# SwiGLU by seven products: where the sums of weight blocks are formed, and where 1/rms is applied

## The chip, the cores and the metric

One core of one Trainium2 chip runs the whole kernel in one launch. The metric is the device time in microseconds of that launch. Before the change three runs took 1748.85 us in the median (1747.3 to 1749.6).

## The reference, cut to what matters

The kernel computes one step of a one-layer decoder for 1024 prompt tokens and 32 sample tokens (T = 1056), model width 1024. The change concerns its last sublayer and the final norm:

```python
def rmsnorm(x, g):
    y = xf * lax.rsqrt(jnp.mean(xf * xf, axis=-1, keepdims=True) + EPS)
    return y * g
def swiglu_ffn(x, g_ffn, w_gate, w_up, w_down):      # D_FF = 2816 = 22 x 128
    h = rmsnorm(x, g_ffn)
    return x + (jax.nn.silu(h @ w_gate) * (h @ w_up)) @ w_down
y = rmsnorm(swiglu_ffn(x, ...), g_final)
```

All of it is float32. Each product is made of three passes of TensorE: both operands are split into a high part (rounded to the format in which TensorE takes 32-bit numbers) and a low rest, and high x high, high x low and low x high are added.

## The kernel before, in words

Data lie with channels on the 128 partitions and tokens along the free axis, so x is 8 blocks of 128 x 1056. The sublayer before leaves x in DRAM (`x3T`) and g x x, split, in SBUF (`x3`); 1/rms of each token, copied to all partitions, is `rbc`. It is applied after the products.

The hidden units are 22 tiles of 128 (f = 0 to 21). `first()` computes tile 0 in the ordinary way. The others go by the seven-product form of Strassen and Winograd: the weights of gate (row 1) and up (row 2), cut in two halves of the width, are four blocks a11, a12, a21, a22 of 128 x 512; the operand, cut in two halves of the width and two halves of the tokens (HT = 528), is B11, b12, B21, B22. Of the weights three sums are needed besides the plain blocks, s1 = a21 + a22 (for product P5), s2 = s1 - a11 (P6), and a11 - a21 (P7), and a12 - s2 (P3); of the operand T1 to T4, made once by `xsums` and `xsums_late` from x read back from DRAM (`xrload`), and each split by `Op.put`. P1 = a11 B11, P2 = a12 B21, P3 = (a12 - s2) B22, P4 = a22 T4, P5 = s1 T1, P6 = s2 T2, P7 = (a11 - a21) T3. One product is 24 matmuls of 264 columns (K = 4 blocks x 3 passes x 2 token quarters).

The down product uses the same form for hidden tiles 0 to 17 (`w_down4`, three groups of three pairs, 12 output tiles "b", K = 3, 18 matmuls a product); the last four tiles and the final norm follow in the ordinary way, in four blocks of tokens, at the end of the body (L1740 on).

`steps` (L1689 on) is the list of products in order: the first two tiles by turns, then one tile at a time in the order P1, P6, P5, P7, P2, P3, P4, then again by turns. Before product s, `ensure(s + 4)` calls `prepare` for the products up to four ahead: GpSimd forms the sum where one is needed (L1497, L1498, L1503, L1509), ScalarE copies the high part (L1517), VectorE subtracts for the low part (L1518, "a split"). The split blocks live in a ring of four (`pslots`), so the fourth one ahead waits for the product before. After the product, `aevac` takes the result from PSUM: P7's two operations (L1572, L1573) read the banks of P7 and P5; P3 and P2 add onto banks that still hold P5 and P1. After P4 the up half is multiplied by 1/rms (L1583) and by the gate half (L1584), both on GpSimd, and `spill` forms the operand sums of the down product for each pair of tiles and stores them to DRAM (`aD`, by GpSimd's DMA queue). The down stage fetches them (`build`, `Op.fetch`, L1387 to L1389) and adds its results onto x (`bevac`, L1631, L1643), which `xsload` reads from `x3T`.

Raw weight blocks are loaded by `pump` (L1485) on the SyncE queue into pages of 128 columns; a block of gate and up takes four pages, one of down three. There are two buffers of 16 pages.

The order of the work: the instructions of the SyncE queue run in the order of the program. Those of all other engines are ordered ahead of time by a planner, which simulates the program with its own costs and takes, on each engine, the ready instruction that is earliest in the program; on the chip each engine then runs its list in that order and waits where it must. `later(n, fn)` and `tick()` put small work, such as 1/rms, behind a number of units of matmuls.

Of the kernel before, what the change touches and what calls it, by code (L numbers as in the profile page):

```python
# [16 lines left out]
P = 128  # L17
# [13 lines left out]
NPAIR, NGRP = 9, 3  # L31
CK = 0.5 * 128.0 ** -0.5
# [105 lines left out]
def body(tc, ctx, I, O):  # L138
# [200 lines left out]
    def rstd(sqs, n, rcol, rbc):  # L339
# [5 lines left out]
        def by_token():  # L345
# [8 lines left out]
            vec.tensor_scalar(v[:, :full], pb[:, :full], 1.0 / D, EPS, ALU.mult, ALU.add)  # L354
            if n % P:
                m = n % P
                vec.tensor_scalar(v[:m, full:full + 1], pb[:m, full:full + 1], 1.0 / D, EPS, ALU.mult, ALU.add)
            y = newton(v[:, :len(tiles)], len(tiles))
# [3 lines left out]
        def over_all(n0=0, size=n):  # L362
            pb = PS[:, 7, :size]
            for j, (o, m) in enumerate(tiles):
                if n0 <= o < n0 + size:
                    mm(pb[:, o - n0:o - n0 + m], y[:m, j:j + 1].to_broadcast([m, P]), ident[:m, :m], True, True)
            act.copy(rbc[:, n0:n0 + size], pb)
# [719 lines left out]
    sqa = ar.take(T)  # L1087
    def residual(xin, src, spill, xout, g, blocks, at_once=False):
# [231 lines left out]

    sqa.drop()
# [92 lines left out]

    def xsums(k):
        x, (t1, t2) = xr[k % 2], (tt2[k % 2][:, a] for a in range(2))
        for a in range(2):
            act.activation(x[:, a], x[:, a], AF.Copy, scale=col(C_GF + k + 4 * a))
# [5 lines left out]
        if k >= 2:  # L1424
            gp.tensor_tensor(x[:, 1, :HT], x[:, 1, :HT], t2, ALU.subtract)
        else:
            ops[T3].put(k, x[:, 0, HT:])
# [3 lines left out]
    def xsums_late():  # L1431
# [5 lines left out]
        for k in (2, 3):  # L1437
            ops[T3].put(k, xr[k % 2][:, 0, HT:])
        for k in (2, 3):
            ops[T4].put(k, xr[k % 2][:, 1, :HT])  # L1440
        for k in (0, 1):
            (h1_, l1_), (h2_, l2_) = ops[B21].ap(k), ops[T2].ap(k)
            a, b = part(U, 2 + k, HT), part(cs, k, HT)
            eng = gp if k else vec
            eng.tensor_tensor(a, h1_, h2_, ALU.subtract)
            eng.tensor_tensor(b, l1_, l2_, ALU.subtract)
            eng.tensor_tensor(a, a, b, ALU.add)
            ops[T4].put(k, a, eng)
# [4 lines left out]
    pages = [(b, i) for b in range(2) for i in range(16)]  # L1453
    wants, held = [], {}

    def room(n):

        for x in pages:
            run = [(x[0], x[1] + i) for i in range(n)]
            if all(y in pages for y in run):  # L1460
                pages[:] = [y for y in pages if y not in run]
# [3 lines left out]
    def at(run):  # L1465
        return wraw[run[0][0]][:, P * run[0][1]:P * (run[-1][1] + 1)]

    def leave(run):
        pages[:] = sorted(pages + run)

    def quarter(kind, i, c, k):

        if kind == "a":
            return I[("w_gate", "w_up")[c]][i][:, 4 * k:4 * k + 4]
        return I["w_down4"][i // 4, i % 4][:, k, c]
# [428 lines left out]
```

## Time and profile before

| | |
|---|---|
| median of three runs | 1748.85 us |
| the profiled execution's own time | 1751.22 us |
| its span | 1749.4 us |
| TensorE (PE) busy | 1678.4 us, 96% |
| VectorE (DVE) busy | 1197.4 us, 68% |
| ScalarE (ACT) busy | 691.9 us, 40% |
| GpSimd (POOL) busy | 572.0 us, 33% |
| mean granted clock of TensorE | 0.981 |
| DMA | 208.03 MB |

The span is the time of the instructions on the chip in one profiled execution; the metric holds a little around it. Busy times are sums over an engine's instructions. A granted clock of 1.0 is the upper of TensorE's two levels, 2.4 GHz, and 0.5 the lower; values between are means over a stretch. The sublayer of the change runs from about 989 us to the end.

### The profile page before, as it was taken

The numbers are of one execution on the slowest core, as the hardware profiler recorded it, in microseconds if no ns is written. First come the engines' busy times: TensorE is split into PE (matmuls) and PEld (weight loads), VectorE is DVE, ScalarE is ACT, GpSimd is POOL, SyncE is SP. The second block draws the span as 40 slices with busy tenths as digits, with TensorE's granted clock in tenths as the row PEclk, the third lists the DMA queues.
The fourth block names the chain that finished last, engine by engine and source line by source line (L and its number), as shares of the span: only waits on it lengthen the run. The fifth ranks groups of instructions, "written<-read, shape, count | busy, mean of one in ns | idle before, by whom it ended". The sixth has DMA issues, their size and how long they took to land. (4 is left out here: it accounts for less than half of the span.)

```text
span 1749.4 us, 32149 instructions
## 1 busy us (share of the span) xinstructions
PE 1678.4 (96%) x12540; PEld 1604.1 (92%) x12540; DVE 1197.4 (68%) x2536; ACT 691.9 (40%) x1396; POOL 572.0 (33%) x509
## 2 busy tenths in 40 slices
PE   6999999999999899999999979999999997999997
PEld 6989999999869899989989979999999997999987
DVE  7787777777638744666554496777677778787666
ACT  5463543543515543344343342222222225244244
POOL 3200100101101323200004375766676653332434
PEclk9999999999999999999999989999999998999999
DMA  5113112112244664475444513222223335544122
GB/s 177 62 34 82 52 55 91 52 51 83 96 148 133 224 205 141 151 241 200 157 147 144 181 38 117 93 92 93 93 98 104 119 106 196 183 156 132 29 101 97
DMA packets 89306, 208.03 MB, mean 119 GB/s; under 512 B 10466, under 2 KB 38018, under 8 KB 89026
## 3 DMA queue, kind: packets, MB, share of 16 engines
q1 hardware_dynamic: 76434, 163.32, 28.5%
q0 software_dynamic: 12720, 42.65, 6.9%
q8 instruction: 99, 1.62, 0.4%
q14 instruction: 53, 0.43, 0.1%
HBM read 158.93 MB, written 47.00 MB: 118 GB/s over the span
## 5 line engine op out<-in xcount | busy, mean ns | idle before, releaser
L266 PE MATMUL banks<-g_all 128*128 128x384 f32 (+7 forms) x4512 | 740.0, 315 | 10.4 <-DVE g_all L415 8.5
L266 PEld LDWEIGHTS banks<-g_all 128*128 128x128 f32 (+1 forms) x4512 | 671.9, 190 | 35.0 <-issue 17.3
L1539 PE MATMUL banks<-g_all 128*128 128x264 f32 x4120 | 560.3, 287 | 22.7 <-DVE f_all L1599 6.6
L1539 PEld LDWEIGHTS banks<-g_all 128*128 128x128 f32 x4120 | 533.6, 191 | 25.0 <-DVE f_all L1599 6.8
L1517 ACT CAST g_all<-f_all 128x512 fp32r<-128x512 f32 (+1 forms) x231 | 134.0, 581 | 358.8 <-PE banks L1539 312.1
L1518 DVE TENSOR_TENSOR g_all<-f_all,g_all 128x512 fp32r<-128x512 f32 (+1 forms) x231 | 237.4, 1036 | 12.7 <-ACT g_all L1517 12.7
L1539 PE MATMUL banks<-g_x,g_all 128*128 128x264 f32 x920 | 168.3, 288 | 8.5 <-DVE g_all L1518 8.5
L1539 PEld LDWEIGHTS banks<-g_x,g_all 128*128 128x128 f32 x920 | 137.4, 192 | 9.2 <-DVE g_all L1518 9.1
L225 DVE TENSOR_TENSOR g_all<-f_all,g_all 128x1024 fp32r<-128x1024 f32 x88 | 109.6, 1247 | 40.9 <-ACT g_all L224 40.4
L224 ACT CAST g_all<-f_all 128x1024 fp32r<-128x1024 f32 x88 | 91.9, 1048 | 96.5 <-PE banks L266 46.5
L1497 POOL TENSOR_TENSOR f_all<-f_all 128x512 f32<-128x512 f32 (+1 forms) x33 | 44.1, 1335 | 151.9 <-DMA f_all<-in_w_down_dram 65.3
L266 PE MATMUL banks<-f_x 128*128 128x129 f32 (+8 forms) x606 | 91.5, 307 | 1.4 <-DVE f_x L726 0.9
L266 PEld LDWEIGHTS banks<-f_x 128*128 128x128 f32 (+4 forms) x606 | 67.1, 159 | 14.9 <-issue 5.7
L1583 POOL TENSOR_TENSOR f_y<-f_y,f_all 128x1056 f32<-128x1056 f32 x21 | 59.4, 2828 | 61.0 <-DVE f_y L1582 61.0
L266 PE MATMUL banks<-g_y,g_all 128*128 128x384 f32 (+1 forms) x432 | 77.6, 323 | 0.0
L1098 DVE TENSOR_TENSOR f_all<-banks,f_all 128x384 f32<-128x384 f32 (+1 forms) x48 | 25.1, 523 | 73.8 <-PE banks L266 73.7
L266 PEld LDWEIGHTS banks<-g_y,g_all 128*128 128x128 f32 x432 | 70.5, 188 | 0.0
L266 PE MATMUL banks<-g_x,g_all 128*128 128x384 f32 (+1 forms) x336 | 70.2, 325 | 0.0
L661 POOL DMA_DIRECT2D mixT<-f_all x23 | 12.9, 562 | 154.6 <-ACT f_all L660 140.6
L266 PEld LDWEIGHTS banks<-g_x,g_all 128*128 128x128 f32 x336 | 57.0, 188 | 0.5 <-issue 0.4
L1099 POOL DMA_DIRECT2D x3T<-f_all x24 | 13.4, 558 | 131.4 <-DVE g_x L1252 84.0
L266 PE MATMUL banks<-f_all 128*32 128x256 f32 (+5 forms) x404 | 42.0, 347 | 14.8 <-DVE f_all L336 6.4
(410 smaller groups left out, 2212.8 us busy)
## 6 DMA issues: line engine op xcount, KB each, us to landing
g_all<-aD SPq DMA_DIRECT2D x48, 264.0 KB, 3.9
f_all<-in_w_mq_dram SPq DMA_DIRECT2D x24, 512.0 KB, 4.3
f_all<-in_w_gate_dram SPq DMA_DIRECT2D x42, 256.0 KB, 2.7
f_all<-in_w_up_dram SPq DMA_DIRECT2D x42, 256.0 KB, 2.7
f_all<-in_w_cm_dram SPq DMA_DIRECT2D x20, 512.0 KB, 3.6
aD<-f_y POOLq DMA_DIRECT2D x18, 528.0 KB, 4.9
f_all<-in_w_down_dram SPq DMA_DIRECT2D x48, 192.0 KB, 3.2
f_all<-in_memK_dram SPq DMA_DIRECT2D x16, 512.0 KB, 5.2
```

Of the source, the lines that this page charges most:

```text
L224: act.copy(R(dst_hi), raw)
L225: eng.tensor_tensor(R(dst_lo), raw, dst_hi, ALU.subtract)
L266: pe.matmul(out, l, r, start=start, stop=stop)
L661: gp.dma_start(mixT[:, 4 + i, P * t:P * t + P], ot)
L1098: vec.tensor_tensor(x, pb[:, :n], t, ALU.add)
L1099: gp.dma_start(spill[:, k, n0:n0 + n], x)
L1497: gp.tensor_tensor(s1, a21, a22, ALU.add)
L1517: act.copy(R(hi), src)
L1518: vec.tensor_tensor(R(lo), src, hi, ALU.subtract)
L1539: pe.matmul(o, x[:, k], R(y[:, n]), start=k == 0 and i == 0 and not more, stop=k == K - 1 and i == 2, skip_group_check=more)
L1583: gp.tensor_tensor(u, u, rbc.ap, ALU.mult)
```

## The change

Three things are changed. (1) The signs of the seven-product form are turned so that all sums of weight blocks are additions (T1 to T3 change sign instead, and the evacuations subtract where they added). The sums are then formed by DMAs that add to what lies at their destination, issued from GpSimd's queue: P5's block is loaded plain with a21 and a22 is added to it; P7's with a11 and a21 is added; P6's with a11 and the finished block of P5 is added, from SBUF to SBUF; P3's with a12 and the finished block of P6 is added. Each product has pages of its own, and the scratch `stmp` of the old sums becomes a third buffer of 16 pages; two of the three are handed out only after the first block of tokens of `first()`. (2) The up half is no longer multiplied by 1/rms. The residual is divided by it instead (`xdivide`, 16 pieces of 128 x 528, one after P5 of each of the tiles 3 to 18, through DRAM to `xS`), so that x / r + down product is r times too small, and the final 1/rms is computed with r taken into account (`times` in `rstd`, from columns saved by `final_by_token`). (3) What GpSimd still did in the loops of this sublayer (operand sums, product of the halves, sums of the spill, last sums of the down stage) goes to VectorE; the operand rows k = 0 and 1 are read from DRAM a second time for it. The sums of squares and one output block of the last part stay on GpSimd.

```diff
@@ rstd
+            parts = [(P, slice(0, full))] + ([(n % P, slice(full, full + 1))] if n % P else [])
+            for m, c in parts:
+                if times is None:
+                    vec.tensor_scalar(v[:m, c], pb[:m, c], 1.0 / D, EPS, ALU.mult, ALU.add)
+                else:
+                    vec.scalar_tensor_tensor(v[:m, c], pb[:m, c], 1.0 / D, times[1][:m, c], ALU.mult, ALU.mult)
...
+            if times is not None:
+                vec.tensor_scalar(v, v, 1.0, EPS, ALU.mult, ALU.add)
+            y = newton(v, len(tiles))
+            if times is not None:
+                vec.tensor_tensor(y, y, times[0][:, :len(tiles)], ALU.mult)
@@ before residual
+    def final_by_token():
+        rfin = fr["y"], fr["y2"] = [ar.take(12)[:, :frow[-1]] for _ in range(2)]
+        pb = PS[:, 7, 496:496 + frow[-1]]
+        for j, (o, m) in enumerate(t for b in ftiles for t in b):
+            mm(pb[:, j:j + 1], sqa[:, o:o + P], one[:, 0:1], True, True)
...
+    def final_over(j):
...
+        act.copy(rbc[:, n0:n0 + n], pb)
@@ residual
         if at_once:
-            by_token, over_all = rstd([sqa[:, :T]], T, None, rbc[:, :T])
-            later(1, by_token)
-            for j, b in enumerate(blocks):
-                later(j + 2, lambda b=b: over_all(*b))
+            later(1, final_by_token)
+            for j in range(len(FBL)):
+                later(2 + j // 2, lambda j=j: final_over(j))
@@ xsums, xsums_late
-        vec.tensor_tensor(t1, x[:, 0, HT:], x[:, 0, :HT], ALU.subtract)
-        gp.tensor_tensor(x[:, 0, HT:], x[:, 1, HT:], x[:, 0, HT:], ALU.subtract)
-        vec.tensor_tensor(t2, x[:, 1, HT:], t1, ALU.subtract)
+        xscale(k)
+        vec.tensor_tensor(t1, x[:, 0, :HT], x[:, 0, HT:], ALU.subtract)
+        vec.tensor_tensor(t2, x[:, 1, HT:], t1, ALU.add)
         ops[T2].put(k, t2)
         ops[T1].put(k, t1)
...
+        for k in (2, 3, 0, 1):
+            x = xr[k % 2]
+            if k < 2:
+                xscale(k)
+            vec.tensor_tensor(x[:, 0, HT:], x[:, 0, HT:], x[:, 1, HT:], ALU.subtract)
+            ops[T3].put(k, x[:, 0, HT:])
+            vec.tensor_tensor(x[:, 1, :HT], x[:, 1, :HT], x[:, 0, :HT], ALU.subtract)
+            vec.tensor_tensor(x[:, 1, :HT], x[:, 1, :HT], x[:, 0, HT:], ALU.add)
+            ops[T4].put(k, x[:, 1, :HT])
+            if k >= 2:
+                xrload(k - 2)
@@ pages, pump, prepare
-    pages = [(b, i) for b in range(2) for i in range(16)]
+    pages = [(wraw[1], i) for i in range(16)]
...
+            put(sy, quarter(*{P1: (0, 0), P6: (0, 0), P7: (0, 0), P2: (0, 1), P3: (0, 1), P5: (1, 0), P4: (1, 1)}[p]))
+            more = {P5: (1, 1), P7: (1, 0)}.get(p)
+            if more:
+                put(gp, quarter(*more), accum_op=ALU.add)
+            other = {P6: P5, P3: P6}.get(p)
+            if other is not None:
+                put(gp, at(held[kind, i, other]).rearrange("p (k c) -> p k c", c=P), accum_op=ALU.add)
...
+        run = held.pop((kind, i, p))
         b = pslots.next()
         hi, lo = b[:, :n], b[:, 512:512 + n]
-        act.copy(R(hi), src)
-        vec.tensor_tensor(R(lo), src, hi, ALU.subtract)
+        act.copy(R(hi), at(run))
+        vec.tensor_tensor(R(lo), at(run), hi, ALU.subtract)
+        leave(run)
         pump()
@@ spill
-            gp.tensor_tensor(c1, e[:, HT:], e[:, :HT], ALU.subtract)
-            vec.tensor_tensor(c2, u[:, HT:], c1, ALU.subtract)
-            gp.tensor_tensor(e[:, HT:], u[:, HT:], e[:, HT:], ALU.subtract)
+            vec.tensor_tensor(c1, e[:, :HT], e[:, HT:], ALU.subtract)
+            vec.tensor_tensor(c2, u[:, HT:], c1, ALU.add)
+            vec.tensor_tensor(e[:, HT:], e[:, HT:], u[:, HT:], ALU.subtract)
             vec.tensor_tensor(c3, u[:, :HT], c2, ALU.subtract)
@@ aevac, P4
-            gp.tensor_tensor(u, u, rbc.ap, ALU.mult)
-            gp.tensor_tensor(u, g, u, ALU.mult)
+            vec.tensor_tensor(u, g, u, ALU.mult)
@@ first
-            vec.tensor_tensor(bu, pu[:, :n], rbc[:, o], ALU.mult)
-            gp.tensor_tensor(u[:, o], z, bu, ALU.mult)
+            vec.tensor_tensor(u[:, o], pu[:, :n], z, ALU.mult)
+            if j == 0:
+                for b in (stmp.ap, wraw[0]):
+                    leave([(b, i) for i in range(16)])
@@ new, and called after P5 of the tiles 3 to 18
+    def xdivide(j):
+        x, n = part(cs, 3, HT), slice(HT * (j % 2), HT * (j % 2) + HT)
+        sy.dma_start(x, x3T[:, j // 2, n])
+        inv = part(ur, j % 2, HT)
+        vec.reciprocal(inv, rbc[:, n])
+        vec.tensor_tensor(x, x, inv, ALU.mult)
+        gp.dma_start(xS[:, j // 2, n], x)
+
     def xsload(d):
-        sy.dma_start(xsb[d], x3T[:, d])
+        sy.dma_start(xsb[d], xS[:, d])
@@ bevac
-                gp.tensor_tensor(x, x, u2, ALU.add)
+                vec.tensor_tensor(x, x, u2, ALU.subtract if p == P3 else ALU.add)
@@ last_ready
-            if wholes_free >= 2 and not wants and len(pages) >= 16:
+            if wholes_free >= 2 and not wants:
@@ body
+            if p == P5 and 3 <= i < 19:
+                xdivide(i - 3)
...
-        by_token, over_all = rstd(sqs, n, None, r)
+        by_token, over_all = rstd(sqs, n, None, r, [fr[x][:, frow[b]:] for x in ("y", "y2")])
```

## Rows read from the trace of the kernel before

**Rows 1.** The page: span, and busy us of each engine (share, instructions).

```profile
span 1749.4 us, 32149 instructions
PE 1678.4 (96%) x12540; PEld 1604.1 (92%) x12540; DVE 1197.4 (68%) x2536; ACT 691.9 (40%) x1396; POOL 572.0 (33%) x509
```

**Rows 2.** Busy time by stretch: length, engines' busy us (instructions), clock, DMA share, GB/s.

```profile
1017.00:1048.00 31.00, 18.51 (x120) 18.27 (x120) 30.11 (x29) 13.42 (x22) 20.97 (x13) 0.78 0.00 1
1048.00:1455.00 407.00, 402.76 (x3300) 401.83 (x3300) 292.94 (x316) 116.95 (x182) 258.87 (x160) 1.00 0.31 106
1455.00:1500.00 45.00, 32.85 (x209) 31.70 (x208) 40.20 (x46) 20.74 (x36) 20.29 (x14) 0.81 0.57 185
1500.00:1677.00 177.00, 174.57 (x1419) 173.83 (x1417) 126.34 (x192) 61.91 (x115) 60.80 (x51) 0.99 0.37 120
1677.00:1687.40 10.40, 7.26 (x35) 7.04 (x36) 7.10 (x11) 5.92 (x9) 1.49 (x2) 0.67 0.60 216
1300.00:1350.00 50.00, 50.00 (x412) 50.00 (x412) 35.83 (x38) 15.00 (x23) 32.59 (x20) 1.00 0.24 82
```

**Rows 3.** TensorE's waits from 985 us on: for what, us in total, times, longest.

```profile
PE banks L1539 <- DVE g_all L1518: 14.1, 6, 5.9
PE banks L1539 <- DVE f_all L1599: 6.6, 1, 6.6
PE banks L1539 <- DVE f_y L1573: 5.7, 5, 2.0
PE banks L1539 <- DVE f_y L1572: 4.9, 1, 4.9
```

**Rows 4.** VectorE's groups, 1050 to 1450: count, busy us, mean ns, idle before, releaser.

```profile
L1518 DVE TENSOR_TENSOR g_all<-f_all,g_all 128x512 fp32r<-128x512 f32 x132 | 161.1, 1233 | 9.7 <-ACT g_all L1517 9.7
L1580 DVE SCALAR_TENSOR_TENSOR f_all<-f_all 128x1056 f32<-128x1056 f32 x19 | 28.1, 1481 | 2.0 <-ACT f_all L1579 2.0
L1575 DVE TENSOR_TENSOR f_all<-banks,f_all 128x528 f32<-128x528 f32 x19 | 13.4, 706 | 13.3 <-PE banks L1539 13.3
```

**Rows 5.** GpSimd's groups, 1050 to 1450, the costliest.

```profile
L1583 POOL TENSOR_TENSOR f_y<-f_y,f_all 128x1056 f32<-128x1056 f32 x19 | 54.9, 2887 | 48.0 <-DVE f_y L1582 48.0
```

**Rows 6.** Line 1518, whole span: count, duration ns min/median/max, first and last start.

```profile
L1518 DVE TENSOR_TENSOR g_all<-f_all,g_all x231: 543/684/5757, 1012.2 to 1670.4; 128x512 fp32r<-128x512 f32 x74, 128x384 fp32r<-128x384 f32 x42
```

**Rows 7.** The reciprocals of lines 514 and 638, same columns.

```profile
L514 DVE RECIPROCAL f_x<-f_x x1: 1142/1142/1142, 69.2 to 69.2; 32x160 f32<-32x160 f32 x1
L638 DVE RECIPROCAL f_all<-f_all x30: 156/164/166, 86.6 to 480.9; 128x1 f32<-128x1 f32 x30
```

**Rows 8.** DMA, 1050 to 1450: packets, MB, share; issues, KB, us to landing.

```profile
q1 hardware_dynamic: 12384, 23.45, 17.2%
f_all<-in_w_up_dram SPq DMA_DIRECT2D x38, 256.0 KB, 2.6
aD<-f_y POOLq DMA_DIRECT2D x18, 528.0 KB, 4.9
aD<-f_y POOLq DMA_DIRECT2D x9, 792.0 KB, 6.9
```

**Rows 9.** Timeline at the start of the products: start us, us, instruction [idle <-releaser].

```profile
1010.42 6.61 PE L266 MATMUL banks<-g_all 128*128 128x288 f32 x48
1016.00 0.38 ACT L367 COPY f_all<-banks 128x288 f32<-128x288 f32 x1
1023.64 8.11 PE L1539 MATMUL banks<-g_all 128*128 128x264 f32 x48 [6.61 <-DVE f_all L1599]
1037.99 0.59 PE L1539 MATMUL banks<-g_x,g_all 128*128 128x264 f32 x1 [5.88 <-DVE g_all L1518]
```

**Rows 10.** The SyncE queue's waits, 1640 to 1680.

```profile
SPq L1653 <- DVE g_all L1518: 29.3, 1, 29.3
```

**Rows 11.** The chain that ended last: start us, us; and one stretch as in rows 2.

```profile
1456.20 4.78 DMA g_all<-aD
...
1485.00:1490.00 5.00, 2.52 (x16) 2.52 (x17) 5.00 (x6) 0.07 (x1) 3.06 (x3) 0.89 0.39 105
```

More of the change, by code (lines that the diff above doesn't have):

```diff
@@ L337, in newton, with rstd @@
         return y
-    def rstd(sqs, n, rcol, rbc):
+    def rstd(sqs, n, rcol, rbc, times=None):
         tiles = [(o, min(P, n - o)) for o in range(0, n, P)]
@@ L1436, in xsums_late @@
             give(x)
[L1437 to L1448, printed above, removed]
+        for k in (2, 3, 0, 1):
[9 more added lines that the diff above has]
+                xrload(k - 2)
     pslots = Ring([gall[:, o:o + 1024] for o in blocks])
-    pages = [(b, i) for b in range(2) for i in range(16)]
+    pages = [(wraw[1], i) for i in range(16)]
     wants, held = [], {}
     def room(n):
[L1458 to L1461, printed above, removed]
+        for j in range(len(pages) - n + 1):
+            run = pages[j:j + n]
+            if run[-1][0] is run[0][0] and run[-1][1] == run[0][1] + n - 1:
+                pages[j:j + n] = []
                 return run
@@ L1465, in at @@
     def at(run):
-        return wraw[run[0][0]][:, P * run[0][1]:P * (run[-1][1] + 1)]
+        return run[0][0][:, P * run[0][1]:P * (run[-1][1] + 1)]
     def leave(run):
[L1469 to L1475, printed above, removed]
+        pages.extend(run)
+        pages.sort(key=lambda p: ([p[0] is b for b in (stmp.ap, wraw[1], wraw[0])].index(True), p[1]))
     def pump():
         while wants:
-            kind, i, c, k = wants[0]
+            kind, i, p = wants[0]
             run = room(4 if kind == "a" else 3)
@@ L1540, in product @@
                               stop=k == K - 1 and i == 2, skip_group_check=more)
+    xS = dram.tile([P, 8, T], F32, name="xS")
     aD = dram.tile([NPAIR, 7, P, HT], F32, name="aD")
@@ L1569, in aevac @@
         elif p == P6:
-            vec.tensor_tensor(two(u2), two(u2), b, ALU.add)
+            vec.tensor_tensor(two(u2), b, two(u2), ALU.subtract)
         elif p == P7:
             vec.tensor_tensor(two(u3), two(u2), b, ALU.add)
-            vec.tensor_tensor(two(u[:, HT:]), two(u3), pair(bank[P5]), ALU.add)
+            vec.tensor_tensor(two(u[:, HT:]), two(u3), pair(bank[P5]), ALU.subtract)
         elif p == P2:
@@ L1576, in aevac @@
         elif p == P3:
-            vec.tensor_tensor(two(g[:, HT:]), two(u2), b, ALU.add)
+            vec.tensor_tensor(two(g[:, HT:]), b, two(u2), ALU.subtract)
             vec.tensor_tensor(g[:, HT:], g[:, HT:], r1, ALU.mult)
@@ L1650, in last_weights @@
         run = room(8)
+        if run is None:
+            return
         raw = at(run)
@@ L1677, in group, with loads @@
         return [(kind, i, p) for p in order for i in tiles]
-    def halves(kind, *tiles):
-        return [(kind, i, c, k) for c, k in ((0, 0), (1, 0), (1, 1), (0, 1)) for i in tiles]
+    def loads(kind, *tiles):
+        out = []
+        for p in (BY_TURNS if len(tiles) > 1 else ALONE):
+            for i in tiles:
+                out += [(kind, i, P5)] if p == P6 else []
+                out += [(kind, i, p)] if p != P5 else []
+        return out
     def banks_alone(x, y, z5, z7):
@@ L1689, in body @@
     steps = group("a", BY_TURNS, 1, 2)
-    wants += halves("a", 1, 2)
+    wants += loads("a", 1, 2)
     bank = {("a", 1): banks_turn(0, 2), ("a", 2): banks_turn(4, 6)}
@@ L1693, in body @@
         steps += group("a", ALONE, f)
-        wants += halves("a", f)
+        wants += loads("a", f)
         bank["a", f] = banks_alone(2, 6, 0, 4)
@@ L1698, in body @@
         steps += group(kind, BY_TURNS, i, i + 1)
-        wants += halves(kind, i, i + 1)
+        wants += loads(kind, i, i + 1)
         bank[kind, i], bank[kind, i + 1] = banks_turn(*x), banks_turn(*y)
```

88 lines of the change are left out of this document (36 added, 52 removed).

## The prediction

> **What bounds the kernel now.** The profiled execution took 1751.2 us, its span 1749.4 [rows 1], so 1.8 us lie outside it; the three timed runs have a median of 1748.85, 2.4 below. I take differences from the profiled execution and subtract them from the median.
>
> I first read the busy times [rows 1]: TensorE holds 96% of the span, so only its idle stretches and its slow-clock stretches can be won. Next the stretches of the last sublayer [rows 2]: 412 matmuls in an undisturbed 50 us make 0.1214 us each. What a stretch took beyond its matmuls at that rate is its loss:
> - start of the products, 1017 to 1048: 31.0 - 120 x 0.1214 = 16.4 us, granted clock 0.78;
> - gate and up tiles, 1048 to 1455: 407 - 3300 x 0.1214 = 6.4 us;
> - change to the down stage, 1455 to 1500: 45 - 209 x 0.1214 = 19.6 us, clock 0.81;
> - rest of the down stage, 1500 to 1677: 177 - 1419 x 0.1214 = 4.7 us;
> - start of the last part, 1677 to 1687.4: 10.4 - 35 x 0.1214 = 6.2 us, clock 0.67.
>
> That is 53 us, all that the change can touch. The waits of TensorE [rows 3] name VectorE for nearly all of it. VectorE is slow there for a reason that its rows show: one split of a weight block takes 0.684 us in the median and up to 5.757 [rows 6], but 1.233 in the mean while GpSimd computes [rows 4], and GpSimd computes 259 of 407 us [rows 2].
>
> **Steady tiles.** A gate/up tile is 168 matmuls, 20.4 us. VectorE does 292.9 us in 407 [rows 2], 14.7 per tile. Afterwards, with GpSimd's arithmetic gone, I take the undisturbed durations: 7 splits x 0.684 = 4.8; seven half-tile operations (six of the kind of L1575 [rows 4], and L1578) x 0.70 = 4.9; the full-width L1580 and the product of the two halves that comes from GpSimd, 2 x 1.48 at most [rows 4], 3.0; four sums of the spill every second tile, 2 x 0.70 = 1.4. GpSimd loses its 2.887 us product with 1/rms [rows 5] and the rest. New is one division piece per tile for 16 tiles: a reciprocal of 528 columns and a product of 0.70. The reciprocal is the dear part: 160 columns took 1.142 us and one took 0.164 [rows 7], so 6.15 ns a column and 0.164 + 527 x 6.15 ns = 3.4 us; were it like any half-tile operation, 0.70. I take 3.4. Sum 4.8 + 4.9 + 3.0 + 1.4 + 4.1 = 18.2 us of 20.4: VectorE goes from 72% to 89% although each operation gets shorter. It still fits, and TensorE stays the bound. A weight block is split four products ahead, so 3 x 2.9 = 8.7 us late is free. The tight place is the seventh sum: the evacuation after P7 (two operations and a split between, 2.1 us) must end within the 2.9 us of P2, since P3 writes on P5's bank. A reciprocal needs only rbc and a free half buffer, free since P3 of the tile before, so the planner can put it into the pause after P3, where nothing waits for it. On tiles with a spill VectorE has about 16 us of work between P3's end and P7's end, 14.5 us later; then a wait of about 1 us can come, 8 times at most. Old waits here gone: up to 6.4. I take a gain of 1 us, from -10 to +6.
>
> **Weight blocks.** Per tile 4 plain loads become 7, and 4 accumulating ones are added, all four on POOL's queue. The trace has no accumulating DMA. Below, an accumulate is a plain 256 KB load, 2.6 us to landing; above, it moves the block three times (source, destination, result), as the 792 KB store by the same queue, 6.9 us [rows 8]. I take twice, as the 528 KB store, 4.9. Engine time goes by 23.45 MB in 17.2% of 400 us [rows 8], 0.341 MB per us for all 16 engines. Per tile: 3 plain x 0.262 = 0.79 MB, accumulates 4 x 0.262 x 2 = 2.10, division pieces in and out 0.54; together 10.1 us in 20.4, a share of 0.49 on top of 0.31 [rows 2]: 0.80 (0.65 to 0.96 at the ends). The Trainium skill (Collectives: The Full Stack, Part 3, "The bandwidth ceiling: the fold count and why AG ≠ RS ≠ AR") says that a reduce needs two source reads on one read ring and so runs at about half of a copy's rate; no run here shows that yet; by it the share would be 0.80 too, and it lowers what I give to the upper end.
>
> Latency has cover. Twelve blocks fit the three buffers, so a load is issued some twelve products, 35 us, before its split. The longest chain is load, P5's accumulate, P6's accumulate: 2.6 + 2 x 4.9 = 12.4 us (16.4 at the upper end). Queued behind a waiting accumulate on POOL are the next accumulates, the spills to aD and the pieces of xS; nobody needs those within a tile. On SP, the load of a division piece waits for the store of the piece before, a tile old.
>
> **Start of the products.** Before, TensorE ended the first tile at 1017.03 and waited 6.61 us, for L1599, and 5.88 us, for a split [rows 9]; the clock was 0.78. The 1/rms of the last block came only at 1016.0 [rows 9]; now two pieces of it go in one turn, so that evacuation can run by 1014, and VectorE's operations shrink from some 1.2 to 0.70. I drop the first wait. But VectorE's half-tile operations grow from 26 to 36, and the loads move: only four blocks are issued before the first tile (P1 of tiles 1 and 2, P5 and P6 of tile 1); all later ones stand on SP, in program order, behind the second reloads of the residual rows. The last of these waits for the late sums of k = 2 and 3, which write where the first tile's operands lie until 1017.0: four splits and three sums each later, about 1021. Two reloads of 1.08 MB take 6.4 us, to 1028 (with latency); P2 of tile 1 lands at 1030 and is split by 1031. P6 of tile 2, with two accumulates, is ready at 1039. Three products end at 1017.0 + 3 x 2.9 = 1025.7. If the planner runs P2 ahead the wait is 5.6 us, if not 13; some 3 us of half clock follow, as behind the old waits. Loss 8 to 16 against 16.4: I take 11, a gain of 5 (-2 to +11).
>
> **Change to the down stage.** Three waits: a fetch from aD that ended at 1461 after 4.78 us of DMA [rows 11], with the DMA engines at 0.57 over the stretch; a sum; and a stretch in which VectorE was busy for all 5 us and TensorE for half [rows 11], with splits beside GpSimd's arithmetic. The second and third, and the half clock after them, some 10 us, are eased by an undisturbed VectorE. The first gets worse: a down tile (126 matmuls, 15.3 us) gains 3 + 8 blocks of 0.196 MB, 6.3 us of DMA time, 0.41 on top of 0.57 [rows 2]: 0.98. I give back 5, a gain of 4 (-8 to +12). The rest of the down stage gets 0.41 on 0.37: 0 (-6 to +3). Start of the last part: the load of the last weights waited 29.3 us for a free buffer [rows 10]; with half more pages and the condition on 16 free ones gone it starts earlier: 2 (0 to 6). Two tiny operations in the final 1/rms (0.3 us) and seven fewer one-column matmuls before the first tile cancel.
>
> Sum: 5 + 1 + 4 + 0 + 2 = 12 us. Forecast 1748.85 - 12 = 1737, for itself 1728 to 1745.
>
> **Rivals.**
> - All VectorE waits go: the planner hides the reloads and the reciprocal, and the old losses shrink from 53 to 25: 1721. For it: no engine but VectorE is named in the long waits. Against: 89% load and a near-full DMA. Chance 0.15.
> - The DMA engines become the limit (slower side). Place: the change to the down stage and, beyond that, every tile. At three times per accumulate the down stage stands at 0.57 + 0.56 = 1.13: 6 us more there, and in-order fetches behind it, some 15 in all, no gain at the start: about 1760. It decides from an accumulate of about three times a plain load; at four a gate/up tile needs 1.11 of its time, 2.2 us x 17, about 1790. For it: 0.57 there already, and a fetch in the chain of waits; against: 0.31 in the tiles. Chance 0.15.
> - The reciprocal lands just before P7's evacuation: up to 3.4 + 0.7 - 0.8 = 3.3 us for each of 16 tiles; at 0.8 each it eats the gain, 1750. Chance 0.12: 0.05 no change, 0.07 slower.
> - It does nothing that lasts: what is won from waits on VectorE is lost to waits on DMA, 1749. 0.10.
> - The start gets no better but the rest goes as forecast: 1743. 0.06.
> - The forecast: 0.42.
>
> Faster by over 0.2% (about what a measurement of this kernel tells from no change): 0.42 + 0.15 + 0.06 = 0.63. Within 0.2%: 0.10 + 0.05 = 0.15. Slower: 0.15 + 0.07 = 0.22. The range 1716 to 1762 leaves out most of the DMA rival's upper half and a little of the best case.
>
> **What would show it.** Splits at a mean near 0.70 in the tiles and GpSimd under a fifth busy show that the contention was the cause. The reciprocal's row should read 3.0 to 3.5 us. Accumulates should land in 3 to 7 us, the DMA share in the tiles rise to 0.65 to 0.96. TensorE's waits at the start should name a split behind a load, not L1599. It is wrong if TensorE waits in the steady tiles for splits behind DMAs, or for the evacuation of P7.

## The result and the profile after

The changed kernel takes 1774.05 us (median of 4 runs, 1773.3 to 1775.1) against 1748.07 for the kernel before in runs beside it: a ratio of 1.0149 [1.0131, 1.0166], slower by 26 us where the prediction said 12 faster. Its profiled execution has a span of 1771.5 us, 22.1 above [rows 1]; that difference is followed below.

The page of the changed kernel, lines as in [rows 1]:

```profile
span 1771.5 us, 32598 instructions
PE 1688.6 (95%) x12548; PEld 1610.8 (91%) x12548; DVE 1181.2 (67%) x2637; ACT 694.4 (39%) x1401; POOL 342.6 (19%) x440
```

GpSimd is freed as planned, from 33% to 19%. VectorE's busy time hardly moved: the division (66.6 us of reciprocals and products) and the product of the two halves taken over from GpSimd (26.4 us) took what the shorter splits of weight blocks gave (237.4 to 146.0 us).

Stretches of the changed kernel, columns as in [rows 2], from the first product of the seven to the last:

```profile
1020.70:1075.00 54.30, 44.90 (x327) 44.04 (x327) 31.05 (x49) 20.24 (x29) 9.96 (x12) 0.91 0.77 206
1075.00:1450.00 375.00, 352.71 (x2826) 351.24 (x2825) 270.76 (x337) 96.78 (x151) 90.62 (x114) 0.98 0.75 202
1450.00:1600.00 150.00, 141.47 (x1104) 138.14 (x1103) 101.80 (x165) 62.34 (x115) 30.23 (x36) 0.98 0.91 253
1600.00:1696.30 96.30, 96.25 (x791) 96.04 (x790) 68.53 (x113) 31.57 (x58) 13.93 (x16) 1.00 0.56 145
```

And the kernel before with the same bounds, from the end of the first tile:

```profile
1017.00:1075.00 58.00, 45.51 (x342) 45.27 (x342) 46.63 (x51) 21.45 (x34) 31.78 (x21) 0.88 0.12 37
1075.00:1450.00 375.00, 370.76 (x3037) 369.83 (x3037) 272.01 (x289) 107.05 (x168) 248.06 (x153) 1.00 0.31 106
1450.00:1600.00 150.00, 135.99 (x1043) 134.64 (x1042) 116.26 (x167) 61.03 (x113) 47.02 (x38) 0.93 0.48 156
1600.00:1676.90 76.90, 76.43 (x625) 75.90 (x624) 54.62 (x78) 23.48 (x42) 33.97 (x27) 1.00 0.28 91
```

The loss of a stretch is, as in the prediction, its length less the matmuls of the products x 0.1214 us; "last part" runs from the last product to the end of the span. Matmuls at a border shift a loss by some tenths. All values are us of profiled executions, one of each kernel; the kernels below the second line are the experiments. A profiled execution can lie some us off its kernel's median (before 3.2 above, after 0.8 below, x3 5.0 above, x5 4.3 below), so differences of that size between two rows of the table say little by themselves.

| kernel | products start | loss to 1075 | 1075 to 1450 | 1450 to 1600 | rest | last part | span |
|---|---|---|---|---|---|---|---|
| before | 1017.0 | 16.6 | 6.3 | 23.4 | 1.0 | 72.5 | 1749.4 |
| after | 1020.7 | 14.7 | 31.9 | 16.0 | 0.3 | 75.2 | 1771.5 |
| x1 division after P2 | 1021.4 | 14.8 | 11.5 | 12.0 | 0.1 | 74.8 | 1747.4 |
| x2 piece loaded earlier | 1019.4 | 15.1 | 5.7 | 12.7 | 0.1 | 73.6 | 1739.3 |
| x3 no accumulates | 1019.4 | 6.1 | 12.6 | 2.0 | 0.1 | 73.8 | 1726.6 |
| x4 no division | 1019.1 | 15.7 | 4.2 | 13.3 | 0.7 | 74.4 | 1740.2 |
| x5 up half on VectorE | 1018.1 | 13.8 | 8.0 | 14.8 | 0.1 | 74.2 | 1741.6 |
| x6 = x1, no accumulates | 1017.6 | 6.4 | 2.1 | 1.4 | 0.1 | 74.6 | 1715.0 |
| x7 = x1, plain copies | 1019.2 | 12.8 | 7.5 | 6.6 | 0.0 | 74.3 | 1733.3 |
| x8 = x1, early loads | 1017.9 | 2.7 | 7.2 | 10.6 | 0.2 | 70.5 | 1721.8 |
| x9 = x2, early loads | 1015.9 | 3.7 | 8.6 | 10.9 | 0.1 | 72.4 | 1724.1 |
| x10 = x9, down sums on GpSimd | 1016.6 | 3.0 | 7.4 | 5.5 | 0.0 | 70.4 | 1715.6 |
| x11 = x10, all SBUF sums | 1017.5 | 2.3 | 4.9 | 9.7 | 0.1 | 70.5 | 1717.6 |

After against before: +3.7 (later start) - 1.9 + 25.6 - 7.4 - 0.7 + 2.7 = 22.0. The steady tiles, where [rows 2] show 6.4 us of loss, lose more than the whole difference. The lines of the changed kernel that matter here: L1517 loads weight blocks (plain on SP's queue, accumulating on GpSimd's), L1534 is ScalarE's copy of the high part (the cast), L1535 VectorE's split, L1555 the matmuls of the products, L1589 and L1590 the evacuation of P7, L1643 to L1647 the division piece. TensorE's waits in the changed kernel from 1015 us on, columns as in [rows 3]:

```profile
PE banks L1555 <- DVE f_y L1590: 23.9, 9, 4.1
PE banks L1555 <- ACT g_all L1534: 8.7, 3, 5.5
PE banks L267 <- ACT g_all L1420: 5.3, 2, 4.3
PE banks L1555 <- DVE g_all L1535: 4.8, 6, 1.6
```

L1590 is the second operation of P7's evacuation, which [rows 3] show under L1573 with 5.7 us. The wait that the prediction removed (L1599 in [rows 3], 6.6 us) is gone. The wait for splits fell from 14.1 to 4.8, but 8.7 us for the casts ahead of them are new. P7's evacuation went from 5.7 to 23.9 us. The line ahead of it on VectorE, L1646, multiplies the division piece with rms (its row: count, duration ns, first and last start; then its idle time in us, times):

```profile
L1646 DVE TENSOR_TENSOR f_y<-f_y,f_all x16: 709/709/711, 1093.1 to 1431.8; 128x528 f32<-128x528 f32 x16
its engine sat idle before it (us, times) until:
  DMA f_y<-x3T: 61.0, 16
```

VectorE stands before this product in every one of 16 tiles for its load from x3T. One such tile, on VectorE, TensorE and SP's queue in turn (start us, us, instruction, [idle <-releaser]):

```profile
1128.28 0.71 DVE L1572 TENSOR_TENSOR f_y<-f_y 128x528 f32<-128x528 f32 x1
1128.90 0.69 DVE L1535 TENSOR_TENSOR g_all<-f_all,g_all 128x512 fp32r<-128x512 f32 x1
1134.40 0.71 DVE L1646 TENSOR_TENSOR f_y<-f_y,f_all 128x528 f32<-128x528 f32 x1 [4.81 <-DMA f_y<-x3T]
1135.03 0.69 DVE L1589 TENSOR_TENSOR f_y<-f_all,banks 128x528 f32<-128x528 f32 x1
...
1136.24 0.70 DVE L1590 TENSOR_TENSOR f_y<-f_y,banks 128x528 f32<-128x528 f32 x1
...
1137.08 1.22 PE L1555 MATMUL banks<-g_all 128*128 128x264 f32 x4 [3.57 <-DVE f_y L1590]
...
1128.82 0.38 SPq L1643 DMA_DIRECT2D f_y<-x3T  x1
1129.62 7.06 SPq L1517 DMA_DIRECT2D f_all<-in_w_gate_dram  x2
```

The product of the piece is written into VectorE's list ahead of P7's evacuation (L1589, L1590). Its load was issued at 1128.82, when VectorE was done with what stood before it at 1129.6; the load landed at about 1134.4, P7's evacuation ended at 1136.9, and TensorE stood for 3.57 us. In the tile before, the same line stands behind L1590 (the last two rows are the end of P3's evacuation and the reciprocal for the tile above):

```profile
1111.40 0.70 DVE L1590 TENSOR_TENSOR f_y<-f_y,banks 128x528 f32<-128x528 f32 x1
1115.93 0.71 DVE L1646 TENSOR_TENSOR f_y<-f_y,f_all 128x528 f32<-128x528 f32 x1 [3.83 <-DMA f_y<-x3T]
...
1118.99 0.70 DVE L1595 TENSOR_TENSOR f_all<-f_all 128x528 f32<-128x528 f32 x1
1119.61 3.45 DVE L1645 RECIPROCAL f_all<-f_all 128x528 f32<-128x528 f32 x1
```

VectorE waits 3.83 us there too, and TensorE waits for nothing. From the second piece on the two orders alternate, so in 7 of the 16 tiles the product stands ahead of P7's evacuation. Between 1075 and 1475 us TensorE waited for L1590 8 times, 22.3 us in all: 2.50 to 4.08 us in each of those 7 tiles (20.9 us), and 1.37 once in the first tile with a piece. The waits also cost clock. The first 27 matmuls behind the five longest took 4.89 to 5.05 us, at a granted clock of 0.67 to 0.69 (a mean between the two levels), and those behind the other three 3.52 to 3.55 us at 1.00, so some 7 us come on top. Together that is 29 of the 31.9 us in the table. One of each:

```profile
1092.36 3.55 PE L1555 MATMUL banks<-g_all 128*128 128x264 f32 x27 [1.37 <-DVE f_y L1590]
...
1137.08 5.05 PE L1555 MATMUL banks<-g_all 128*128 128x264 f32 x27 [3.57 <-DVE f_y L1590]
```

DMA of the changed kernel, 1075 to 1475, columns as in [rows 8]:

```profile
q0 software_dynamic: 16366, 41.23, 43.1%
q1 hardware_dynamic: 21696, 40.15, 31.7%
f_all<-f_all POOLq DMA_DIRECT2D x36, 256.0 KB, 4.7
f_all<-in_w_up_dram POOLq DMA_DIRECT2D x35, 256.0 KB, 6.2
f_all<-in_w_up_dram SPq DMA_DIRECT2D x34, 256.0 KB, 3.5
f_y<-x3T SPq DMA_DIRECT2D x16, 264.0 KB, 6.6
```

A 264 KB load takes 6.6 us to landing in this traffic, where a 256 KB one took 2.6 [rows 8].

### The profile page after: what moved, and what is told of

It reads as the page before. It is cut to its first block, busy times and chain, and to the rows that moved or that the text cites. A ratio compares the mean times of both kernels' runs of the same rounds, so it can differ in the third digit from the quotient of the medians.

```text
span 1771.5 us, 32598 instructions
## 1 busy us (share of the span) xinstructions
PE 1688.6 (95%) x12548; PEld 1610.8 (91%) x12548; DVE 1181.2 (67%) x2637; ACT 694.4 (39%) x1401; POOL 342.6 (19%) x440
## 3 DMA queue, kind: packets, MB, share of 16 engines
q0 software_dynamic: 33008, 78.44, 17.9%
## 5 line engine op out<-in xcount | busy, mean ns | idle before, releaser
L267 PE MATMUL banks<-g_all 128*128 128x384 f32 (+6 forms) x4560 | 750.0, 315 | 16.9 <-DVE g_all L422 8.3
L1555 PE MATMUL banks<-g_all 128*128 128x264 f32 x4128 | 583.2, 289 | 33.9 <-DVE f_y L1590 23.9
L1555 PEld LDWEIGHTS banks<-g_all 128*128 128x128 f32 x4128 | 545.6, 193 | 38.7 <-issue 23.0
L1534 ACT CAST g_all<-f_all 128x512 fp32r<-128x512 f32 (+1 forms) x231 | 132.5, 579 | 342.5 <-PE banks L1555 249.3
L1555 PE MATMUL banks<-g_x,g_all 128*128 128x264 f32 x912 | 175.8, 287 | 6.3 <-ACT g_all L1534 5.5
L1535 DVE TENSOR_TENSOR g_all<-f_all,g_all 128x512 fp32r<-128x512 f32 (+1 forms) x231 | 146.0, 637 | 19.3 <-ACT g_all L1534 19.3
L1555 PEld LDWEIGHTS banks<-g_x,g_all 128*128 128x128 f32 x912 | 141.2, 190 | 7.2 <-ACT g_all L1534 5.7
L1517 POOL DMA_DIRECT2D f_all<-f_all x66 | 59.6, 908 | 223.2 <-DVE g_all L1535 37.4
L267 PEld LDWEIGHTS banks<-f_x 128*128 128x128 f32 (+4 forms) x606 | 67.4, 160 | 14.8 <-issue 5.7
L267 PE MATMUL banks<-g_x,g_all 128*128 128x384 f32 (+3 forms) x352 | 75.1, 324 | 0.0
L1128 DVE TENSOR_TENSOR f_all<-banks,f_all 128x384 f32<-128x384 f32 (+1 forms) x48 | 25.1, 523 | 73.8 <-PE banks L267 73.8
L267 PEld LDWEIGHTS banks<-g_y,g_all 128*128 128x128 f32 x432 | 70.4, 188 | 0.0
L1517 POOL DMA_DIRECT2D f_all<-in_w_up_dram x42 | 40.1, 975 | 133.6 <-DMA f_all<-in_w_up_dram 63.5
L1421 DVE TENSOR_TENSOR g_all<-g_all 128x528 fp32r<-128x528 f32 x56 | 39.0, 707 | 30.1 <-ACT g_all L1420 29.9
L267 PE MATMUL banks<-f_all 128*32 128x256 f32 (+4 forms) x412 | 43.2, 342 | 14.8 <-DVE f_all L351 4.6
L1420 ACT CAST g_all<-g_all 128x528 fp32r<-128x528 f32 x56 | 35.2, 633 | 52.9 <-DMA g_all<-aD 50.5
```

Source lines behind the costliest of these rows:

```text
L267: pe.matmul(out, l, r, start=start, stop=stop)
L1128: vec.tensor_tensor(x, pb[:, :n], t, ALU.add)
L1420: act.copy(R(hi), lo)
L1421: vec.tensor_tensor(R(lo), lo, hi, ALU.subtract)
L1517: dma.dma_start(at(run).rearrange("p (k c) -> p k c", c=P), src, **how)
L1534: act.copy(R(hi), at(run))
```

## The experiments

Theory: the 25.6 us are the load of the division's piece, late, multiplied by the place of its product ahead of P7's evacuation. Rivals: VectorE's added work as such; the accumulates' DMA traffic as such. The time of each run is followed by its ratio to the kernel before, measured beside it, with the 95% interval.

**x1, the division's call two products later.**

```diff
-            if p == P5 and 3 <= i < 19:
+            if p == P2 and 3 <= i < 19:
                 xdivide(i - 3)
```

> The call of the division piece stands after P2 instead of after P5; nothing else differs. Theory A (place in VectorE's list): the product of a division piece waits 3.2 to 4.8 us for its load in all 16 tiles, but costs TensorE only where it stands ahead of P7's evacuation, as in half of them. Here it stands behind it in all: the 22.3 us of waits for L1590 and the half clock after them go, the product still waits some 4 us each: 1745 to 1753 us. Rival B (the DMA engines are the limit): the wait only moves to another operation, 1768 to 1776 us.

1749.2 us, 1.0011 [0.9997, 1.0025]: 25 us back, with the same instructions. VectorE still stands for the piece's load, 67.3 us in all; TensorE's waits for L1590 fall to 5.0. The idle time costs only where it lies ahead of P7's evacuation. VectorE's work is the same as in the changed kernel, so that work as such is not the cause.

**x3, no accumulating DMAs** (the sums of weight blocks are left out).

```diff
-            if more:
+            if False:
...
-            if other is not None:
+            if False:
```

> The accumulating DMAs are left out (the weights of P5, P6, P7 and P3 are the first blocks alone); the division stays after P5. Rival B: the DMA share in the tiles falls from 0.75 to about 0.4, the load of a division piece lands in about 3 us instead of 6.6, its product waits under 1.5 us, and both the 22 us in the tiles and the 8.4 us at the start go: 1738 to 1746. If the load is late because SyncE issues it late, behind loads that wait for pages, the product still waits over 2.5 us and only the start is won: 1762 to 1768.

1723.33 us, 0.9861 [0.9835, 0.9887]: below both ranges expected. The piece's load lands in 3.8 us then and its wait falls from 61.0 to 43.6 us, so part of this is the first stall again; x6 below takes the two apart.

**x4, no division; x5, the up half's product with 1/rms on VectorE instead.** In x4 the residual is not divided (left out of the computation); x5 computes all, with the sums still accumulated.

```diff
-            if p == P5 and 3 <= i < 19:
-                xdivide(i - 3)
...
-        sy.dma_start(xsb[d], xS[:, d])
+        sy.dma_start(xsb[d], x3T[:, d])
```

And in x5 alone:

```diff
+            vec.tensor_tensor(u, u, rbc.ap, ALU.mult)
             vec.tensor_tensor(u, g, u, ALU.mult)
```

> No division pieces at all (the residual is not divided, the final norm is unchanged), xsload reads x3T. Theory A: as x1, since what the pieces cost TensorE is the wait alone: 1744 to 1752. Rival C (VectorE is too full, the reciprocals of 3.45 us cost too): 1730 to 1742, well under x1.

> The division is undone: the up half is multiplied by 1/rms again, on VectorE (one more full-width operation per tile, 1.25 us by the undisturbed row), the final norm as before the change; the accumulating DMAs stay. Theory A: 1744 to 1752, as x4. Rival C: 1 to 5 us above x4, since the operation stands in VectorE's list in every tile.

x4: 1742.84, 0.9972 [0.9955, 0.9988]. x5: 1747.76, 0.9994 [0.9978, 1.0009]. Without the division 31 us are back. x4's time lies between its two ranges and decides neither. x5 has the first and third part of the change, sums by DMA and GpSimd's work on VectorE, and they move nothing that these runs can tell; what the second part is worth, x2 shows.

**x2, the piece's load issued after P1**, the product left in its place after P5.

```diff
+            if p == P1 and 3 <= i < 19:
+                j = i - 3
+                sy.dma_start(part(cs, 3, HT), x3T[:, j // 2, HT * (j % 2):HT * (j % 2) + HT])
...
-        sy.dma_start(x, x3T[:, j // 2, n])
```

> The load of the division's piece is issued after P1 of the same tile, two products before the reciprocal that used to follow it; everything else as in the changed kernel, the product with the piece still stands after P5's evacuation. The load landed 6.6 us (median) after its issue and the product with it waited 0.84 to 4.8 us; issued about 12 us earlier it is there in time. Theory A (TensorE lost 22 us in the tiles because VectorE stood at the product with the piece, whose load was late, ahead of P7's evacuation): the waits of that line go, TensorE's waits for P7's evacuation fall from 23.9 us to under 7, and the time is 1748 to 1753. Theory B (the 1.35 us of work of reciprocal's companions and the general load on VectorE, 67% busy, make P7's evacuation late, not the load): nothing goes, 1770 to 1775. Theory C (SP reaches the load no earlier, since weight loads that wait for pages stand before it in program order): the wait shrinks in part, 1758 to 1768.

1742.82 us, 0.9967 [0.9953, 0.9981]: 31 us less than the changed kernel by moving one load, and below every number expected. In the table 26 of them are in the tiles; the rest, up to 3 us in a stretch, was not followed. A tile as above, on VectorE and on SP's queue:

```profile
1129.14 0.70 DVE L1572 TENSOR_TENSOR f_y<-f_y 128x528 f32<-128x528 f32 x1
1129.89 0.71 DVE L1645 TENSOR_TENSOR f_y<-f_y,f_all 128x528 f32<-128x528 f32 x1
...
1133.23 0.70 DVE L1589 TENSOR_TENSOR f_y<-f_all,banks 128x528 f32<-128x528 f32 x1 [1.64 <-PE banks L1555]
...
1126.68 0.38 SPq L1754 DMA_DIRECT2D f_y<-x3T  x1
1128.03 6.86 SPq L1517 DMA_DIRECT2D f_all<-in_w_gate_dram  x4
```

The product (L1645 here) is still ahead of L1589, but finds its data, and it is VectorE that now waits for TensorE. Not as I had reckoned: the load is no 12 us earlier. It stands in SP's queue among weight loads that wait for pages, which the splits give back (x2, 1075 to 1475 us):

```profile
SPq L1517 <- DVE g_all L1535: 319.1, 130, 7.6
```

So it goes out only about 3 us earlier, measured from P6's evacuation (1.2 us ahead of L1587 instead of 1.8 behind it). It lands within 3.2 us, with the next gate loads queued behind it, where the one of the changed kernel took about 5.6 right behind two. Its wait fell from 61.0 us to 3.1 in the whole run. So the lateness of one load, with its product ahead of P7's evacuation, is the cause: either remedy takes most of the tiles' loss away (31.9 us, then 11.5 in x1 and 5.7 in x2, against 6.3 before). x2 equals x4, so the division itself costs nothing then, and it stands 5 us below x5, which has the up half's product with 1/rms on VectorE in its place (the two intervals just overlap).

**x6 and x7: what an accumulate costs.** On top of x1, x6 has no accumulates; x7 keeps their DMAs as plain copies (both leave the sums out).

```diff
-                put(gp, quarter(*more), accum_op=ALU.add)
+                put(gp, quarter(*more))
```

> The division after P2, and no accumulating DMAs: the sums of the weight blocks are left out, the plain loads of one block each stay. Each edit alone gave 1749 (division after P2) and 1723 (no accumulates) against 1774. Theory A (the two costs overlap: 43% of the wait for the piece's load came from the accumulates' traffic, and the stall in the tiles was counted in both): 1710 to 1720. Theory B (they are independent): 1774 - 25 - 51 = 1698. Theory C (once the accumulates are gone the division's place is worth nothing): 1721 to 1725. By stages against the run with the division after P2: start 14.8 to 6, tiles 11.5 to 5, stretch 1450 to 1600 us 12 to 2, start of the products 2 us earlier, last part 1 us less: 28 us, 1721.

> The division after P2; the accumulating DMAs of the sums of weight blocks stay where they are, on the same queue with the same source, size and target, but overwrite instead of adding, so the sums are left out. It parts the cost of transferring more from the cost of adding in the transfer. Theory A (the accumulation itself is dear: it keeps the DMA engines longer than a plain transfer of the same bytes): the DMA share between 1075 and 1475 us falls from 0.78 to under 0.65, the time to 1725 to 1738. Theory B (only the number of transfers, their bytes and GpSimd's issue count): the share stays near 0.75, and the time within 3 us of 1749.

x6: 1716.52, 0.9809 [0.9786, 0.9832]. x7: 1735.18, 0.9921 [0.9902, 0.994]. The costs overlap, as theory A of x6 said: 32.7 us for the accumulates beside x1, not 51. Of these, 18.7 (x7 less x6) are transfers and issues, 14.0 (x1 less x7) are the adding; the time of x7 is in its theory A's range. GpSimd's queue between 1075 and 1475 us in x1, x7 and x6, in this order (packets, MB, share):

```profile
q0 software_dynamic: 17276, 42.45, 45.0%
```

```profile
q0 software_dynamic: 11984, 41.84, 28.9%
```

```profile
q0 software_dynamic: 5824, 21.63, 14.6%
```

The accumulates hold the DMA engines for 45.0 - 14.6 = 30.4% of the stretch, plain copies of the same blocks for 14.3%: 2.1 times as long. They move about the same bytes (20.8 against 20.2 MB) in 11452 packets against 6160. The share of all DMA in the tiles, 0.78 in x1, is 0.65 in x7, where theory A wanted less. By the table, the accumulates' cost lies at the start (14.8 to 6.4), in the turn to the down products (12.0 to 1.4) and in the tiles (11.5 to 2.1).

**x8, three loads earlier; x9, the same with the division after P5.** x8 is x1 with x2's load; weight loads go out as soon as pages are free, ahead of the residual's reloads; and the last part's four weight blocks get pages of their own.

```diff
                     leave([(b, i) for i in range(16)])
+                pump()
...
         raw = at(run)
-        leave(run)
         sy.dma_start(raw, I["w_down"][j].rearrange("p k c -> p (k c)"))
```

> The whole computation. The division after P2, its piece loaded after P1; weight loads of the first tiles issued as soon as their pages are free, ahead of the reloads of the residual on SP, so that the accumulates of the second tile start earlier; the loads of the last part's four weight blocks each in pages of its own, so that they don't wait for one another. Against 1749 of the division after P2 alone: the start loses 14.8 us, of which TensorE's waits for the casts of late sums are 8 to 9: gain 4 to 8. The tiles lose 11.5 us, of which the waits for P7's evacuation are 5: gain 2 to 5. The last part waits 4.3 us for its first activations: gain 2 to 4. Theory A (these are real and not covered by something next in line): 1733 to 1741. Theory B (DMA engines, 0.78 to 0.93 busy, only shift the same waits elsewhere): 1746 to 1751.

> The early loads of the run before (1723.5), with the division left after P5 as in the changed kernel. Its piece, loaded after P1, is there when VectorE comes to it. Theory A (with the load in time the division's place after P5 is at least as good as after P2; 1742.8 stood against 1749.2 without the other two loads): 1714 to 1722. Theory B (that difference came from chance in the start and the turn to the down products): 1723 to 1727. Theory C (place alone makes P7's evacuation late): over 1735.

x8: 1723.48, 0.9853 [0.9832, 0.9875]. x9: 1724.33, 0.9858 [0.9839, 0.9877]. x8 is below both of its ranges. Its start loses 2.7 us in place of 14.8 in x1, more than I gave it, and its clock is 1.00 in place of 0.90, so the half clock behind the waits went too; the last part gains 4 (1 in x9). With the load early the division's place is worth nothing that these runs can tell (0.9 us): theory B of x9. The start of the changed kernel, GpSimd's queue, then SP's:

```profile
1034.57 0.86 POOL L1517 DMA_DIRECT2D f_all<-in_w_up_dram  x1 [24.85 <-DMA f_all<-in_w_up_dram]
...
1024.25 2.55 SPq L1445 DMA_DIRECT2D f_y<-x3T  x2
1026.90 0.54 SPq L1517 DMA_DIRECT2D f_all<-in_w_up_dram  x1
```

The first plain load that an accumulate needs goes out at 1026.90, behind the reloads (L1445); GpSimd stands 24.85 us for it. The changed kernel has issued two accumulates when TensorE ends the first tile. In x8 it is eight, and no wait of TensorE for L1534 is left; the fourth and the last of the eight on GpSimd's queue:

```profile
1011.69 0.87 POOL L1517 DMA_DIRECT2D f_all<-f_all  x1 [2.11 <-PE banks L267]
...
1017.92 0.86 POOL L1517 DMA_DIRECT2D f_all<-f_all  x1 [0.86 <-DMA f_all<-f_all]
```

**x10 and x11, some sums back on GpSimd.** x9, with the sums of two blocks that both lie in SBUF added by GpSimd: in the down products (x10), in all (x11).

```diff
+            if other is not None and kind == "b":
+                gp.tensor_tensor(at(run), at(run), at(held[kind, i, other]), ALU.add)
-            if other is not None:
+            elif other is not None:
                  put(gp, at(held[kind, i, other]).rearrange("p (k c) -> p k c", c=P), accum_op=ALU.add)
```

> As the run beside it, but in the down products the sum of two blocks that both lie in SBUF is added by GpSimd (128x384 elements) instead of by an accumulating DMA. Theory A (between 1450 and 1600 us the DMA engines, 0.87 busy, set the loss of 10.6 us, and leaving out a third of the accumulates there takes some): 3 to 7 us below the run beside it. Theory B (GpSimd's sums slow VectorE's splits, 634 ns without such sums and 1036 ns in the kernel before, and the fetched operands are VectorE's work too): 0 to 5 us above it.

> As the run before it (1717.4), but in the gate and up products too the sum of two blocks that both lie in SBUF (128x512) is added by GpSimd; only sums with a block from DRAM are still accumulating DMAs. Theory A (the DMA engines, 0.79 busy in these tiles, are off the critical path once the loads are early: the tiles lose 7 to 9 us with them): 1714 to 1720. Theory B (GpSimd's sums lengthen VectorE's splits by 90 ns each, as in the down products, and VectorE is the next limit in the tiles): 1720 to 1728. Theory C (a lower DMA share shortens the wait of 3.6 us and others for P7's evacuation): 1708 to 1713.

x10: 1717.42, 0.9825 [0.981, 0.9839], the fastest version here that computes everything, 7 us below x9 as theory A said. x11: 1718.29, 0.9818 [0.9793, 0.9844], the same as x10. GpSimd's sums in x10, 1450 to 1600 us, then VectorE's splits there in x10 and, in the fence behind, in x9 (count, busy us, mean ns, idle before):

```profile
L1525 POOL TENSOR_TENSOR f_all<-f_all 128x384 f32<-128x384 f32 x18 | 20.3, 1186 | 51.9 <-DMA f_all<-in_w_down_dram 24.2 <-DVE g_all L1537 17.5 <-ACT g_x L1420 6.4
...
L1537 DVE TENSOR_TENSOR g_all<-f_all,g_all 128x384 fp32r<-128x384 f32 x67 | 42.9, 642 | 3.1 <-ACT g_all L1536 3.1
```

```profile
L1535 DVE TENSOR_TENSOR g_all<-f_all,g_all 128x384 fp32r<-128x384 f32 x64 | 35.1, 549 | 3.0 <-ACT g_all L1534 2.9
```

Each split gets 93 ns longer, and still the stretch loses 5.5 us in place of 10.9, with a DMA share of 0.76 in place of 0.87. That the share is the reason is not shown: x11, with the same edit in the down products and a share of 0.75, loses 9.7 there. What is shown is the time of the runs: 6.9 us between x9 and x10, which differ in the down sums alone, and nothing that can be told between x10 and x11, so in the tiles the trade is even.

## Why the prediction was wrong

The step that failed is in the steady tiles. The prediction put the reciprocal's place and VectorE's load there (89%), named the tight place, P7's evacuation within P2, and then passed the piece's load with "On SP, the load of a division piece waits for the store of the piece before, a tile old". It asked when the buffer is free, not when SP comes to the load and when the load lands in the traffic that the same change brings. The runs showed that load landing 6.6 us (median) after its issue, VectorE idle for it 61.0 us, and TensorE waiting 2.5 to 4.1 us behind it in 7 tiles. Both ends were in the prediction's own numbers: a DMA share of 0.80, and SP's loads going out in program order. The gain of 1 us became a loss of 25.6; the bound of -10 did not hold it. The sign that it gave for being wrong, a wait for the evacuation of P7, is what came.

Term by term, after against before, and in x2, which has the change without that stall:

- Steady tiles, +1: -25.6; in x2 +0.6. The reciprocal lies behind P3's evacuation, as predicted, and takes 3.45 us where 3.4 stood. VectorE's work in a tile with a piece comes to 17.7 us by x2's durations, where 18.2 stood, so its load was not what failed:

```profile
L1645 DVE RECIPROCAL f_all<-f_all x16: 3445/3447/3454, 1082.0 to 1413.5; 128x528 f32<-128x528 f32 x16
```

- VectorE's durations, undisturbed 0.684: splits took 0.686 in the mean in the changed kernel's tiles, against 1.233 [rows 4]. That fits GpSimd's arithmetic as what lengthened them. The only run that brings part of it back into the tiles, x11 with 45.2 us of GpSimd's sums in 375, has 0.734; the whole step was not tested by itself.

```profile
L1535 DVE TENSOR_TENSOR g_all<-f_all,g_all 128x512 fp32r<-128x512 f32 x126 | 85.6, 686 | 4.3 <-ACT g_all L1534 4.3
```

- Accumulates at twice a plain load's DMA time, a share of 0.80 in the tiles: 2.1 times (x1, x6, x7) and 0.75, 0.80 in x2. The Trainium skill (Collectives: The Full Stack, Part 3, "The bandwidth ceiling: the fold count and why AG ≠ RS ≠ AR") gives the reduce of a collective about half of a copy's rate; the 2.1 times of the accumulates here agree. Landing came to 4.7 and 6.2 us where 4.9 stood.
- Start of the products, +5: +1.9, in x2 +1.5. The mechanism was right: L1599's wait went, loads stand behind the reloads, and a late sum is waited for. The waits were 2.93 and 5.46 us, for the cast of such a sum, where I had 5.6 in one (5.3 by the two times that I gave).
- Change to the down stage and its rest, +4: +8.1 (7.4 + 0.7), in x2 +11.6. VectorE undisturbed seems to have been worth more than I gave, although the DMA share is 0.91 and the accumulates still cost about 11 us there (x1 against x6).
- Last part, +2: -2.7, in x2 -1.1. The load of the last weights goes out 18.5 us before the products end, where it was 16.3, so it does start earlier. But the four loads shared one set of pages, each waiting for the load and the split before it, and took 17.9 us instead of 14.0. The fetch of the last activations stood behind them and went out 0.5 us before the products end instead of 2.2, as SP's queue in the changed kernel shows:

```profile
1677.75 17.93 SPq L1682 DMA_DIRECT2D f_all<-in_w_down_dram  x4
1695.77 3.79 SPq L1419 DMA_DIRECT2D g_all<-aR  x7
```

- Before the first tile, 0: -3.7. "Seven fewer one-column matmuls" was miscounted; there are 22, the kernel before has 18, and the broadcasts grew from 18 to 22. Between them, in the changed kernel:

```profile
996.76 6.00 PE L267 MATMUL banks<-g_all 128*128 128x384 f32 x24
```

The added matmuls cost 1.4 us. Another 1.5 is the row shown: these 24 matmuls took 6.00 us, at a granted clock of 0.94 over 975 to 1000, and 4.46 at 1.00 in x2, x5 and x8, whose instructions there are the same (in x1, x3, x4 and x9 6.0 again). The remaining 0.8 arose earlier, in code that the change leaves alone; the start of the products varies from 1015.9 to 1021.4 over the kernels of the table.

Without that stall the forecast would have been about half right in size: x2's profiled spans give a gain of 10 us (1749.4 - 1739.3), its medians 6 (1749.17 - 1742.82), against 12, and its time lies inside the range of the forecast. Its terms would have been partly luck: the start gave 1.5 where 5 stood, the down stage 11.6 where 4 stood. Of the rivals, the third named the place, "just before P7's evacuation", and a price of up to 3.3 us a tile; it had the reciprocal there, and it was the product with its load, 2.5 to 4.1 us in every second tile. The second, DMA engines as the limit, was not what made the change slower, since x1 and x2 with the same traffic are level with the kernel before or faster. But the traffic helped to make that load late (without accumulates it lands in 3.8 us), and it costs 32.7 us beside x1 by itself.

## What to carry to other kernels

For each operation that a change adds to an in-order list, ask when its operand lands, in the traffic after the change, and what stands behind it in that list; its own duration is the small part (0.71 us here, against up to 4.8 of waiting). A load is as late as the loads that wait for space ahead of it in program order: issuing one three microseconds earlier was worth 31 us, and loads issued ahead of the reloads at the start of a stage another 12. Work moved to DMA shortens an engine's list and still has a price: the accumulates cost 32.7 us beside leaving them out. Against an idle GpSimd doing the sums of blocks in SBUF, they were even in the tiles (x10, x11) and 7 us worse in the down products (x9, x10).

## What the traces show of the hardware

- An accumulating DMA of 256 KB between SBUF tiles landed in 4.7 us, one from DRAM in 6.2, where plain loads took 3.5 beside them; accumulates hold the DMA engines 2.1 times as long as plain copies of the same blocks (30.4% against 14.3% of 400 us in x1, x7 and x6).
- VectorE's reciprocal took 3.45 us for 528 columns, 6.5 ns a column, five times a product of the same size (0.71); 3.4 was forecast from two smaller ones.
- GpSimd's sum of 128x384 took 1.19 us and lengthened VectorE's splits of that size only from 549 to 642 ns (x9, x10); its sums of 128x512, 1.33 us each, those of 128x512 from 684 to 734 ns (x10, x11). In the kernel before, with GpSimd busy 259 of 407 us, they took 1233 ns in the mean.
